# A decoder trunk on one core: three groups of two chunks per channel mixer computed as 2x2 block products in seven products

## The chip, the cores and the metric

The kernel runs on one core of a Trainium2 chip. The metric is the device time of one execution in microseconds (us); lower is better. Before the change the median of three runs is 585.55 us (585.5 to 585.72).

## The reference

Two layers over x (256 positions, 1024 channels). Each layer has a token mixer (layer 0: gated chunks, layer 1: block attention, both beside an attention into 256 memory tokens), then a channel mixer, each closed by a layer norm of 4^(1/4) x + f(x). The change concerns the channel mixer:

```
def swiglu(x, w_in, w_out):          # w_in: 1024 x 5632, w_out: 2816 x 1024
    g, u = jnp.split(x @ w_in, 2, axis=-1)
    return (jax.nn.silu(g) * u) @ w_out
```

All arrays are fp32.

## The kernel before

**Precision.** Every large product takes operands in two parts: hi, the value rounded to the matmul format, and lo, the rest. `split` (L142) makes them with one ScalarE cast (L143) and one VectorE subtraction (L144); the product is the sum of three passes, hi·hi, hi·lo and lo·hi.

**Weights.** `Stream` (L76) brings the weights in units of 128 partitions x 2048 columns (1 MB) in the fixed order of `weight_units` (L42): SyncE loads a unit into one of 3 raw buffers, `piece` (L101) splits it in steps of 512 columns into one of 5 split buffers, and a unit's buffer is free again when TensorE has used all of it. The buffers set how far ScalarE and VectorE may run ahead of TensorE.

**Channel mixer** (`Ffn`, L445). The 2816 hidden channels are 11 chunks of 256. For a chunk, gate (`g`) and value (`f`) are each computed with the weights as the stationary operand: `ws_wide` (L227) issues, for two column blocks and eight row blocks, one matmul of 512 columns (hi of the weight against hi and lo of x) and one of 256 (lo of the weight against hi of x), 32 in all. `projected` (L459) adds the two halves of the PSUM tile (L466, L467) and applies silu to the gate (L470); `chunk_in` (L473) multiplies (L476) and splits the result into `ht`. `chunk_out` (L512) multiplies `ht` with the chunk's output weights `w`, 24 matmuls of 512 columns into four PSUM accumulators, one chunk behind. In layer 1 the first two chunks have the positions on the partitions instead (`chunk_in_tm`, L481), half by half as x becomes ready.

**Order.** TensorE's instructions run in the order in which the program writes them. ScalarE, VectorE and SyncE get an order from the scheduler of the tile framework when the program is built, and each then runs its own list strictly in order. The main loop of layer 0 is

```
for c in range(NFF):
    ffn.chunk_in(c)
    if 1 <= c <= NFF - 3:
        ffn.chunk_out(c - 1)
```

Of the kernel before, what the change touches and what calls it, by code (L numbers as in the profile page):

```python
# [33 lines left out]
RAW_BUFS = 3  # L34
SPLIT_BUFS = 5
# [5 lines left out]

def weight_units():  # L42

    u = [(f"v{i}", 2 * W_MIX) for i in range(4)]
    u += [(n, 2048) for n in ("qm0", "u0", "u1", "u2", "km0", "vm0")]
    u += [(f"o0_{i}", 2048) for i in range(4)]
    u += [("km1", 2048), ("vm1", 2048)]
    u += ffn_units(0, 1)
    u += [(f"bv{i}", 2 * W_MIX) for i in range(4)]
    u += [("qm1", 2048)]  # L50
    u += [(f"qk{i}", 2048) for i in range(6)]
    u += [(f"o1_{i}", 2048) for i in range(4)]
    u += ffn_units(1, 1)
    return u


def ffn_units(l, ahead):

    u = []
    for c in range(NFF):  # L60
        u += [(f"g{l}_{c}", 2048), (f"f{l}_{c}", 2048)]
        if c >= ahead and c <= NFF - 3:
            u += [(f"w{l}_{c - ahead}", 2048)]
    u += [(f"w{l}_{c}", 2048) for c in range(NFF - 3, NFF)]
    return u
# [10 lines left out]
class Stream:  # L76


    def __init__(self, nc, rawp, splp, wflat, split, first):
        self.nc, self.rawp, self.splp, self.wflat, self.split = nc, rawp, splp, wflat, split  # L80
        self.units = weight_units()
        self.names = [n for n, _ in self.units]
        self.raw, self.hl = {}, {}
        self.loaded = self.split_u = first
        self.pos = 0
        self.finished = set()
        self.oldest = 0

# [4 lines left out]
    def load_ahead(self):  # L93
        while self.loaded < len(self.units) and self.loaded < self.split_u + RAW_BUFS:
            name, n = self.units[self.loaded]
            raw = self.rawp.tile([P, 2048], F32, tag="raw", name=f"raw_{name}")
# [4 lines left out]
    def piece(self):  # L101

        if self.split_u >= len(self.units) or self.split_u >= self.oldest + SPLIT_BUFS:
            return False
        self.load_ahead()
        name, n = self.units[self.split_u]
        if self.pos == 0:
            self.hl[name] = self.splp.tile([P, 2, 2048], F32R, tag="spl", name=f"spl_{name}")
        step = 512 if n == 2048 else 768
        hl, raw, c = self.hl[name], self.raw[name], self.pos  # L110
        self.split(hl[:, 0, c:c + step], hl[:, 1, c:c + step], raw[:, c:c + step])
        self.pos += step
        if self.pos == n:
            self.pos = 0
            self.split_u += 1
            self.load_ahead()
        return True

    def get(self, name):
        i = self.names.index(name)  # L120
        while self.split_u <= i:
            assert self.piece(), name
        return self.hl[name]

    def done(self, name):
        self.finished.add(name)
        while self.oldest < len(self.names) and self.names[self.oldest] in self.finished:
            self.oldest += 1


def build(nc, tc, ins, out):
    ET = mybir.EngineType
    with (
        tc.tile_pool(name="const", bufs=1) as const,
        tc.tile_pool(name="raw", bufs=RAW_BUFS) as rawp,
        tc.tile_pool(name="spl", bufs=SPLIT_BUFS) as splp,
# [27 lines left out]
        stream = Stream(nc, rawp, splp, ins["w"], split, first=4)  # L164

        def mm(o, lhsT, rhs, start, stop):
            nc.tensor.matmul(o, lhsT, rhs, start=start, stop=stop)  # L167
# [26 lines left out]
        for i in range(4):  # L194
            raw = rawp.tile([P, 2048], F32, tag="raw", name=f"raw_v{i}")
            hl = splp.tile([P, 2, 2048], F32R, tag="spl", name=f"spl_v{i}")
            for k in range(2):
                kk = 2 * i + k
                nc.sync.dma_start(xraw[:, kk, :], ins["xT"][kk * P:(kk + 1) * P, :])
                nh = 2 if kk == 0 else 1  # L200
                cuts = [(k * W_MIX + h * W_MIX // nh, k * W_MIX + (h + 1) * W_MIX // nh) for h in range(nh)]
                for c0, c1 in cuts:
                    nc.sync.dma_start(raw[:, c0:c1], stream.unit_ap(f"v{i}")[:, c0:c1])
                split(xT[:, kk, 0, :], xT[:, kk, 1, :], xraw[:, kk, :])
                for c0, c1 in cuts:
                    split(hl[:, 0, c0:c1], hl[:, 1, c0:c1], raw[:, c0:c1])
                w = hl[:, :, :2 * W_MIX].rearrange("p s (k c) -> p s k c", k=2)
                for h in range(2):
                    for n, (a, b) in enumerate(PASSES):
                        for tt in range(2):  # L210
                            mm(va[tt][h][:, :384], xT[:, kk, a, tt * P:(tt + 1) * P], w[:, b, k, h * 384:(h + 1) * 384],
                               kk == 0 and n == 0, kk == KT - 1 and n == 2)
            stream.done(f"v{i}")
# [4 lines left out]
        def ws_proj(pst, w, xs, cols=(0, 1)):  # L218

            wv = w.rearrange("p s (k c) -> p s k c", k=KT)  # L220
            for j in cols:
                for k in range(KT):
                    for n, (a, b) in enumerate(PASSES):
                        mm(pst[:, j % pst.shape[1], :], wv[:, a, k, j * P:(j + 1) * P], xs(b, k),
                           k == 0 and n == 0, k == KT - 1 and n == 2)

        def ws_wide(pst, w, xs, j):  # L227


            wv = w.rearrange("p s (k c) -> p s k c", k=KT)  # L230
            for k in range(KT):
                for b in ((0, 1) if k == 0 else (1, 0)):
                    mm(pst[:, :T] if b else pst, wv[:, b, k, j * P:(j + 1) * P],
                       xs(0, k) if b else flat(xs(slice(None), k)), k == 0 and b == 0, k == KT - 1 and b == 0)
# [38 lines left out]
        def transpose_x(tt, xres, xT_new, nm):  # L273
            for h in range(2):
                pt = mm_tile(f"pt{nm}{tt}{h}")
                for k in range(4):
# [3 lines left out]
                      pt.rearrange("p (k t) -> p k t", k=4))  # L280

# [60 lines left out]
        def mem_v(name, memx):  # L342

            w = stream.get(name)
            wv = w.rearrange("p s (k c) -> p s k c", k=KT)
# [3 lines left out]
            def part(tt):  # L349
                for k in range(KT):  # L350
                    ts_pass(t[:, tt, :], lambda a: memx(a, k), lambda b: wv[:, b, k, :], tt, k == 0, k == KT - 1)
# [32 lines left out]
        def proj_t(name, xs):  # L384
            t = mm_tile(f"h{name}").rearrange("p (j t) -> p j t", j=2)
            ws_proj(t, stream.get(name), xs)
# [34 lines left out]
        class OutProj:  # L421
# [4 lines left out]
            def term(self, tt, k):  # L426
                def rhs(b, c0, c1):
                    w = stream.get(f"o{self.l}_{k // 2}").rearrange("p s (k c) -> p s k c", k=2)
                    return w[:, b, k % 2, c0:c1]
# [15 lines left out]
        class Ffn:  # L445
            def __init__(self, l, xs, xres, nm):
                self.l, self.xs, self.xres, self.nm = l, xs, xres, nm
                self.hts, self.acc = {}, None
# [10 lines left out]
            def projected(self, unit, name):  # L459

                s = work_tile(f"s{name}")
                for j in range(2):
                    p = mm_tile(f"p{name}{j}")
                    ws_wide(p, stream.get(unit), self.xs, j)
# [3 lines left out]
                stream.done(unit)  # L468
                if unit[0] == "g":
                    nc.scalar.activation(s, s, AF.Silu)  # L470
                return s

            def chunk_in(self, c):  # L473
                l, nm = self.l, self.nm
                sg, su = (self.projected(f"{w}{l}_{c}", f"{n}{nm}{c}") for w, n in (("g", "g"), ("f", "u")))
                nc.vector.tensor_mul(sg, sg, su)  # L476
                ht = self.ht_tile(c)
                src = sg.rearrange("p (k t) -> p k t", k=2)
                split(ht[:, 0], ht[:, 1], src)

            def chunk_in_tm(self, c, tt, pt, part):  # L481

                name = f"{'gf'[part]}{self.l}_{c}"
                w = stream.get(name).rearrange("p s (k c) -> p s k c", k=KT)
                for k in range(KT):
                    ts_pass(pt[:, part * 256:part * 256 + 256], lambda a: self.xs(a, k), lambda b: w[:, b, k, :], tt,
# [19 lines left out]
            def term(self, c, k, tt):  # L506
                def rhs(b, c0, c1):
                    w = stream.get(f"w{self.l}_{c}").rearrange("p s (k c) -> p s k c", k=2)
                    return w[:, b, k, c0:c1]
                return lambda a: self.hts[c][:, a, k, tt * P:(tt + 1) * P], rhs  # L510

            def chunk_out(self, c, last=False):  # L512
                for tt in range(2):
                    for k in range(2):
                        acc_mms(self.acc[tt], *self.term(c, k, tt), c == 0 and k == 0, last and tt == 1 and k == 1)
                stream.done(f"w{self.l}_{c}")

            def end_tile(self, tt, mid=None):

                for c in range(NFF - 3, NFF - 1):  # L520
# [34 lines left out]
        stream.get("qm0")  # L555
# [9 lines left out]
        wsT = actp.tile([P, 2, D], F32, tag="xres", name="wsT").rearrange("p a c -> p (a c)")[:, :12 * P]  # L565
# [5 lines left out]
        bsB = actp.tile([P, 6, P], F32, tag="bsB", name="bsB")  # L571
        for j in range(2):
            nc.sync.dma_start(bsB[j * HD:(j + 1) * HD, :, :], ins["bs"][j:j + 1, :, :].to_broadcast([HD, 6, P]))

        qm = mem_q("qm0", xs)
        vn = actp.tile([P, 2, W_MIX], F32, tag="vbig", name="vn")
# [7 lines left out]
        for i in range(3):  # L584
            pu = mm_tile(f"pu{i}").rearrange("p (j t) -> p j t", j=2)
            ws_proj(pu, stream.get(f"u{i}"), xs)
# [17 lines left out]
        for jj in range(3):  # L604
# [7 lines left out]
            bias = bsB[:, 2 * jj:2 * jj + 2, :].rearrange("p (j o) t -> p j o t", o=1).to_broadcast([P, 2, 2, P])  # L612
# [28 lines left out]
        transpose_x(0, xres, x1T, "a")  # L641
# [3 lines left out]
        transpose_x(1, xres, x1T, "a")  # L645
        vm_part(1)
        ffn = Ffn(0, x_of(x1T), xres, "f")
        for c in range(NFF):
            ffn.chunk_in(c)
            if c == 1:  # L650
# [216 lines left out]
```

## Time and profile before

| | |
|---|---|
| median of 3 runs | 585.55 us |
| the profiled execution, its own time | 586.11 us |
| its span, first to last instruction | 584.4 us |
| TensorE matmul busy | 572.7 us (98%) |
| VectorE busy | 415.7 us (71%) |
| ScalarE busy | 331.8 us (57%) |
| moved by DMA | 110.55 MB, 189 GB/s mean |
| mean granted TensorE clock | 0.998 |

The profile is of one execution; 1.7 us of its own time lie outside the span. Busy time of an engine counts an instruction's whole length, and instructions of one engine may overlap at their ends. A chain is the work that ended last, followed back step by step to what released it.

### The profile page before, as it was taken

The page shows a single profiled execution, that of the slowest core. Times are in us where ns is not written, and L with a number is a line of the kernel's source. Part 1 is how long each engine was busy: PE and PEld are TensorE (multiplying, and loading weights), DVE is VectorE, ACT ScalarE, POOL GpSimd, SP SyncE. Part 2 cuts the span into 40 slices and gives each one's busy share as a digit, 9 for nine tenths or more (in the row PEclk, how much of TensorE's full clock was granted, in tenths as well). Part 3 has the DMA queues.
Part 4 walks back from the last instruction along what each step waited for, and adds up shares of the span by engine and source line. Part 5 has one row for each costly group of instructions (what it writes and reads, how often), then busy time and mean ns, then how long its engine had stood idle before and what let it go on. Part 6 is the DMA issues. An engine that isn't in the chain of part 4 may idle for free.

```text
span 584.4 us, 9071 instructions
## 1 busy us (share of the span) xinstructions
PE 572.7 (98%) x3496; PEld 508.4 (87%) x3496; DVE 415.7 (71%) x783; ACT 331.8 (57%) x718; POOL 14.7 (3%) x22
## 2 busy tenths in 40 slices
PE   7999999999999999999999999999999999999995
PEld 7999979888888888888999899789988888888884
DVE  5788989866556557565988887497766566566637
ACT  6767957755545545553468888464646455455410
POOL 1030000000000000000100000000000000000001
PEclk9999999999999999999999999999999999999999
DMA  8996557755545645545386324128735545555002
GB/s 295 354 347 247 189 219 242 288 201 201 216 165 195 216 170 190 173 151 181 117 297 236 131 87 145 73 72 283 290 149 215 182 179 216 183 180 180 34 1 72
DMA packets 19867, 110.55 MB, mean 189 GB/s; under 512 B 2160, under 2 KB 4976, under 8 KB 8432
## 3 DMA queue, kind: packets, MB, share of 16 engines
q1 hardware_dynamic: 19536, 109.72, 52.2%
q8 instruction: 27, 0.44, 0.3%
q10 hardware_dynamic: 288, 0.26, 0.1%
q14 instruction: 16, 0.13, 0.1%
HBM read 108.92 MB, written 1.05 MB: 188 GB/s over the span
## 4 chain that ended last, share of the span: by engine, by line
PE 95%; DVE 2%; DMA 1%; ACT 0%; issue 0%; SPq 0%; POOLq 0%
PE puf L167 11%; PE pgf L167 11%; PE fof L167 10%; PE fog L167 9%; PE pug L167 9%; PE pgg L167 9%; PE qk L167 5%; PE tm L167 4%; PE opc L167 4%; PE opa L167 4%; PE pu L167 3%; PE bv L167 3%; PE pvm L167 3%; PE va L167 2%; PE hqm L167 2%; PE hkm L167 2%
## 5 line engine op out<-in xcount | busy, mean ns | idle before, releaser
L143 ACT CAST spl_f<-raw_f 128x512 fp32r<-128x512 f32 x88 | 48.7, 619 | 43.6 <-issue 32.7
L144 DVE TENSOR_TENSOR spl_f<-raw_f,spl_f 128x512 fp32r<-128x512 f32 x88 | 55.5, 685 | 23.3 <-ACT spl_f L143 23.2
L167 PE MATMUL puf<-x1T,spl_f 128*128 128x256 f32 (+1 forms) x352 | 63.3, 337 | 0.0
L167 PE MATMUL pgf<-x1T,spl_g 128*128 128x256 f32 (+1 forms) x352 | 63.3, 337 | 0.0
L144 DVE TENSOR_TENSOR spl_w<-raw_w,spl_w 128x512 fp32r<-128x512 f32 x88 | 56.7, 688 | 7.1 <-ACT spl_w L143 5.6
L167 PE MATMUL fof<-spl_w,htf 128*128 128x512 f32 x264 | 61.6, 390 | 0.0
L167 PEld LDWEIGHTS pgf<-x1T,spl_g 128*128 128x128 f32 x352 | 54.4, 188 | 8.1
L167 PEld LDWEIGHTS puf<-x1T,spl_f 128*128 128x128 f32 x352 | 54.4, 188 | 7.9
L144 DVE TENSOR_TENSOR spl_g<-raw_g,spl_g 128x512 fp32r<-128x512 f32 x88 | 56.7, 686 | 4.1 <-ACT spl_g L143 3.5
L167 PEld LDWEIGHTS fof<-spl_w,htf 128*128 128x128 f32 x264 | 49.5, 188 | 10.0
L143 ACT CAST spl_w<-raw_w 128x512 fp32r<-128x512 f32 x88 | 49.8, 619 | 9.3 <-issue 5.0
L167 PE MATMUL fog<-spl_w,htg 128*128 128x512 f32 x228 | 53.2, 389 | 0.0
L143 ACT CAST spl_g<-raw_g 128x512 fp32r<-128x512 f32 x88 | 49.8, 621 | 5.0 <-PE tm L167 2.5
L167 PE MATMUL pgg<-x3T,spl_g 128*128 128x512 f32 (+1 forms) x288 | 51.9, 338 | 0.0
L167 PE MATMUL pug<-x3T,spl_f 128*128 128x512 f32 (+1 forms) x288 | 51.8, 337 | 0.0
L167 PEld LDWEIGHTS pgg<-x3T,spl_g 128*128 128x128 f32 x288 | 44.5, 188 | 6.6
L167 PEld LDWEIGHTS fog<-spl_w,htg 128*128 128x128 f32 x228 | 42.7, 188 | 8.6
L167 PEld LDWEIGHTS pug<-x3T,spl_f 128*128 128x128 f32 x288 | 44.5, 188 | 6.5
L167 PE MATMUL qk<-x2T,spl_qk 128*128 128x256 f32 x288 | 37.0, 285 | 0.0
L167 PEld LDWEIGHTS qk<-x2T,spl_qk 128*128 128x128 f32 x288 | 35.2, 191 | 0.6 <-issue 0.6
L466 ACT COPY sgf<-pgf 128x256 f32<-128x256 f32 x22 | 8.2, 373 | 29.3 <-PE pgf L167 29.3
L467 DVE TENSOR_TENSOR sgf<-sgf,pgf 128x256 f32<-128x256 f32 x22 | 9.3, 421 | 21.1 <-ACT sgf L466 20.9
(187 smaller groups left out, 893.3 us busy)
## 6 DMA issues: line engine op xcount, KB each, us to landing
raw_g<-in_w SPq DMA_DIRECT2D x22, 1024.0 KB, 4.9
raw_f<-in_w SPq DMA_DIRECT2D x22, 1024.0 KB, 4.8
raw_w<-in_w SPq DMA_DIRECT2D x22, 1024.0 KB, 4.8
raw_o<-in_w SPq DMA_DIRECT2D x8, 1024.0 KB, 4.9
raw_qk<-in_w SPq DMA_DIRECT2D x6, 1024.0 KB, 4.9
raw_u<-in_w SPq DMA_DIRECT2D x3, 1024.0 KB, 7.0
raw_bv<-in_w SPq DMA_DIRECT2D x4, 768.0 KB, 4.4
raw_v<-in_w SPq DMA_DIRECT2D x7, 384.0 KB, 5.3
```

The costliest lines, as they stand in the source:

```text
L143: nc.scalar.copy(hi, src)
L144: nc.vector.tensor_sub(lo, src, hi.bitcast(F32))
L167: nc.tensor.matmul(o, lhsT, rhs, start=start, stop=stop)
L466: nc.scalar.copy(sl, p[:, T:])
L467: nc.vector.tensor_add(sl, sl, p[:, :T])
```

## The change

Three times per channel mixer two chunks `c` and `c+1` form a group (`S` in the plan below; `P` is a chunk as before, `T` one of the two chunks of layer 1 with positions on the partitions). The group's left operand is x as 2x2 blocks (positions 0 to 127 and 128 to 255, channels 0 to 511 and 512 to 1023), its right operand the 1024 x 1024 weights as 2x2 blocks (gate and value columns): four raw units of 1 MB named 11, 12, 21, 22. Their product is formed in seven block products M1 to M7 instead of eight. Each is 12 matmuls in `product`, with x as the stationary operand and 512 weight columns moving.

- The left operands that are sums are made once per layer from fp32 copies of x (`transpose_x` keeps them, `sums` adds and splits).
- The right operands that are sums are made in `make`, in place in the raw unit, by VectorE, one half unit at a time, before the half is split: M5, M6, M7 and M4 take one addition per half.
- The products of a group come out with positions on the partitions, so its two `ht` tiles take eight TensorE transposes (step `tp`), run inside the next chunk.
- All weights are now split in halves of 1024 columns into 9 half buffers; a half is freed by itself. There are 4 raw buffers, and the units 11 and 21 lie in two activation tiles (`gb` and `vbig`) instead.
- The mixer's norm vectors are loaded at the last chunk (before: at chunk 4), since unit 11 uses their tile; layer 0's spatial bias comes with six transfers instead of two.
- TensorE's order in a mixer is the list that `ffn_steps` returns.

```
+RAW_BUFS = 4
+HALF_BUFS = 9
+PLAN = ((("P", 0), ("S", 1), ("P", 3), ("S", 4), ("P", 6), ("P", 7), ("S", 8), ("P", 10)),
+        (("T", 0), ("T", 1), ("S", 2), ("P", 4), ("S", 5), ("P", 7), ("S", 8), ("P", 10)))
+PRODUCTS = ("M1", "M5", "M2", "M3", "M6", "M7", "M4")
+OPERAND = {"M1": ("11", None), "M5": ("11", "12"), "M2": ("21", None), "M3": ("22", None),
+           "M6": ("11", "22"), "M7": ("12", "22"), "M4": ("21", "11")}
...
+def ffn_steps(l):
+    steps, prev = [], []
+    for kind, c in PLAN[l]:
+        outs = [("out", p, k, (0, 1)) for p in prev for k in range(2)]
...
+        if kind == "P":
+            ins = [("in", c, w, x) for w in "gf" for x in range(2)]
...
+            steps += [ins[0], ("tp",), ins[1], *outs[:n // 2], ins[2], *outs[n // 2:max(n // 2, n - 1)], ins[3],
+                      *outs[max(n // 2, n - 1):]]
+        else:
+            ins = [("s", c, m) for m in PRODUCTS]
+            steps += [*ins[:5], outs[0], ins[5], outs[1], ins[6]]
...
+    def make(self):
...
+        raw = self.raw[parts[0]][:, sl]
+        if len(parts) == 2:
+            self.nc.vector.tensor_add(raw, raw, self.raw[parts[1]][:, sl])
+        hl = self.splp.tile([P, 2, 1024], F32R, tag="spl", name="spl_" + "_".join(map(str, key)))
+        self.split(hl[:, 0, :n], hl[:, 1, :n], raw)
...
+            def sums(self, A):
+                a11, a12, a21, a22 = A[0, 0], A[0, 1], A[1, 0], A[1, 1]
+                nc.vector.tensor_sub(a22, a22, a21)
+                nc.vector.tensor_sub(a21, a11, a21)
+                nc.vector.scalar_tensor_tensor(a11, a11, -1.0, a22, ALU.mult, ALU.subtract)
+                nc.vector.scalar_tensor_tensor(a12, a12, -1.0, a11, ALU.mult, ALU.subtract)
...
+                    split(hl[0], hl[1], a)
...
+            def product(self, c, m):
...
+                dst = {"M1": self.X, "M6": self.X, "M7": self.X, "M4": self.X, "M2": self.Y}.get(m, self.Z)
...
+                for x in range(2):
+                    w = stream.get(f"s{self.l}_{c}", m, x)
+                    for k in range(2):
+                        for n, (a, b) in enumerate(PASSES):
+                            mm(dst, self.left[m](a, 2 * x + k), w[:, b, k * 512:(k + 1) * 512],
...
+                if m == "M1":
+                    self.m1 = kept("m1", self.X)
+                elif m == "M5":
+                    self.m5 = kept("m5", self.Z)
+                elif m == "M2":
+                    nc.vector.tensor_add(self.m1, self.m1, self.Y)
+                    nc.scalar.activation(self.m1, self.m1, AF.Silu)
+                elif m == "M6":
+                    u2 = kept("u2", self.X)
+                    nc.vector.tensor_add(u2, u2, self.Z)
+                    nc.vector.scalar_tensor_tensor(self.m1, self.m1, -1.0, u2, ALU.mult, ALU.mult)
+                elif m == "M7":
+                    nc.vector.tensor_add(self.m5, self.m5, self.X)
+                elif m == "M4":
+                    sg = work_tile(f"sg{self.nm}{c}")
+                    nc.scalar.activation(sg, self.X, AF.Silu)
+                    nc.vector.scalar_tensor_tensor(self.m5, self.m5, -1.0, sg, ALU.mult, ALU.mult)
...
         ffn = Ffn(0, x_of(x1T), xres, "f")
-        for c in range(NFF):
-            ffn.chunk_in(c)
...
+        stream.held.clear()
+        ffn.sums(A)
+        gb = ffn.run()
```

The order in which the engines' instructions stand moves with this. In the lists below `raw_` and `spl_` are the raw and split forms of a weight, with layer, chunk or group, product and half in the name (`spl_s0_1_M5_0`: layer 0, group 1, product M5, half 0; `raw_s0_1_11`: its unit 11); `Aa` are the fp32 copies of x, `Sf` their split sums, `sgf`, `sff`, `suf` gate and value of a chunk, `m1` and `m5` the two results of a group; a size ends the row.

VectorE before, where layer 0's channel mixer begins, from the last pieces of x on (L144 split, L467 addition of a projection's halves):

```order
L144 TENSOR_TENSOR x1T_1014<-pta11_1203,x1T_1014 128x4x128
L377 TENSOR_TENSOR klm_128<-hkm1_1087,kkm11_1086 64x256
L144 TENSOR_TENSOR spl_g0_1_1342<-raw_g0_1_1168,spl_g0_1_1342 128x512 x2
L144 TENSOR_TENSOR spl_f0_1_1393<-raw_f0_1_1246,spl_f0_1_1393 128x512 x4
L144 TENSOR_TENSOR spl_w0_0_1449<-raw_w0_0_1297,spl_w0_0_1449 128x512 x2
L467 TENSOR_TENSOR sgf0_1235<-sgf0_1235,pgf00_1236 128x256
```

VectorE now at the same place, after the first two sums of x (L219 split, L176 addition of two weight units, L540 and L541 the other sums of x, L555 addition of a projection's halves):

```order
L219 TENSOR_TENSOR spl_s0_1_M1_0_1342<-raw_s0_1_11_1234,spl_s0_1_M1_0_1342 128x1024
L540 SCALAR_TENSOR_TENSOR Aa00_1057<-Aa00_1057,Aa11_1185 128x512
L219 TENSOR_TENSOR SfM51_1217<-Aa11_1185,SfM50_1216 128x512
L541 SCALAR_TENSOR_TENSOR Aa01_1066<-Aa01_1066,Aa00_1057 128x512
L219 TENSOR_TENSOR SfM61_1225<-Aa00_1057,SfM60_1224 128x512
L219 TENSOR_TENSOR SfM71_1229<-Aa10_1176,SfM70_1228 128x512
L219 TENSOR_TENSOR SfM31_1221<-Aa01_1066,SfM30_1220 128x512
L555 TENSOR_TENSOR sgf0_1282<-sgf0_1282,pgf00_1232 128x256
L219 TENSOR_TENSOR spl_s0_1_M1_1_1351<-raw_s0_1_11_1234,spl_s0_1_M1_1_1351 128x1024
L555 TENSOR_TENSOR sgf0_1282<-sgf0_1282,pgf01_1233 128x256
L176 TENSOR_TENSOR raw_s0_1_11_1234<-raw_s0_1_11_1234,raw_s0_1_12_1236 128x1024 x2
L176 TENSOR_TENSOR raw_s0_1_12_1236<-raw_s0_1_12_1236,raw_s0_1_22_1240 128x1024
```

The four sums of x, their four splits and three weight additions now stand between x and the second product's weights.

VectorE now, around the end of layer 0's second group (L606 the addition of M7 into m5, L610 the last product of the group):

```order
L606 TENSOR_TENSOR m5f4_1756<-m5f4_1756,Xf4_1713 128x512
L219 TENSOR_TENSOR spl_g0_6_1_1937<-raw_g0_6_1699,spl_g0_6_1_1937 128x1024
L219 TENSOR_TENSOR spl_w0_4_0_1964<-raw_w0_4_1849,spl_w0_4_0_1964 128x1024
L219 TENSOR_TENSOR spl_w0_4_1_1979<-raw_w0_4_1849,spl_w0_4_1_1979 128x1024
L219 TENSOR_TENSOR spl_f0_6_0_1998<-raw_f0_6_1851,spl_f0_6_0_1998 128x1024
L219 TENSOR_TENSOR spl_w0_5_0_2017<-raw_w0_5_1863,spl_w0_5_0_2017 128x1024
L610 SCALAR_TENSOR_TENSOR m5f4_1756<-m5f4_1756,sgf4_1897 128x512
L219 TENSOR_TENSOR spl_f0_6_1_2032<-raw_f0_6_1851,spl_f0_6_1_2032 128x1024
```

Five splits of later weights stand ahead of the product that finishes the group. Before, a chunk's own product had no weights of this kind between it and the value projection: VectorE's rows there were

```order
L467 TENSOR_TENSOR suf2_1535<-suf2_1535,puf20_1536 128x256
L467 TENSOR_TENSOR suf2_1535<-suf2_1535,puf21_1566 128x256
L476 TENSOR_TENSOR sgf2_1484<-sgf2_1484,suf2_1535 128x512
L144 TENSOR_TENSOR spl_g0_4_1766<-raw_g0_4_1635,spl_g0_4_1766 128x512 x2
L144 TENSOR_TENSOR htf2_1586<-sgf2_1484,htf2_1586 128x512
```

## Rows read from the trace of the kernel before

**Rows 1.** The page: span, and busy time of each engine.

```profile
span 584.4 us, 9071 instructions
PE 572.7 (98%) x3496; PEld 508.4 (87%) x3496; DVE 415.7 (71%) x783; ACT 331.8 (57%) x718; POOL 14.7 (3%) x22
```

**Rows 2.** Busy time by stretch; columns: PE, PEld, DVE, ACT, POOL, PEclk, DMA share, GB/s.

```profile
102.40:286.20 183.80, 183.80 (x978) 157.61 (x977) 121.68 (x209) 96.94 (x194) 0.99 (x1) 1.00 0.53 189
391.70:415.00 23.30, 23.30 (x199) 23.30 (x198) 19.26 (x37) 12.28 (x24) 0.99 (x1) 1.00 0.69 242
```

**Rows 3.** The chain that ended last, layer 0's mixer: start, us, what.

```profile
98.69 0.87 PE pta L277 x8
...
102.43 5.59 PE pgf L167 x32
108.02 5.59 PE puf L167 x32
113.61 5.59 PE pgf L167 x32
...
124.80 5.44 PE fof L167 x24
```

**Rows 4.** The same chain where layer 1's mixer leaves its first two chunks.

```profile
416.23 5.47 PE fog L167 x24
421.70 0.22 PE tpg L500 x2
421.92 4.20 PE pgg L167 x24
```

**Rows 5.** VectorE in order of time: start, us, line, operation, count.

```profile
84.11 2.49 DVE L144 TENSOR_TENSOR spl_vm<-raw_vm,spl_vm 128x512 fp32r<-128x512 f32 x4
86.51 1.89 DVE L144 TENSOR_TENSOR spl_g<-raw_g,spl_g 128x512 fp32r<-128x512 f32 x3
...
288.05 0.94 DVE L144 TENSOR_TENSOR spl_bv<-raw_bv,spl_bv 128x768 fp32r<-128x768 f32 x1
288.91 0.20 DVE L262 BATCH_NORM_AGGREGATE mvf<-stf 128x2 f32<-128x12 f32 x1
...
290.97 1.41 DVE L269 SCALAR_TENSOR_TENSOR xres<-xres,rsf,gb0ffn 128x512 f32<-128x512 f32 x2
292.30 1.89 DVE L144 TENSOR_TENSOR spl_qm<-raw_qm,spl_qm 128x512 fp32r<-128x512 f32 x3
...
401.46 1.28 DVE L144 TENSOR_TENSOR x3T<-ptc,x3T 128x512 fp32r<-128x512 f32 x2
```

**Rows 6.** Groups of instructions, each shape apart: count, busy us, mean ns, idle before.

```profile
L144 DVE TENSOR_TENSOR spl_f<-raw_f,spl_f 128x512 fp32r<-128x512 f32 x88 | 55.5, 685 | 23.3 <-ACT spl_f L143 23.2
L467 DVE TENSOR_TENSOR sgf<-sgf,pgf 128x256 f32<-128x256 f32 x22 | 9.3, 421 | 21.1 <-ACT sgf L466 20.9
L476 DVE TENSOR_TENSOR sgf<-sgf,suf 128x512 f32<-128x512 f32 x11 | 7.6, 692 | 0.4
L144 DVE TENSOR_TENSOR spl_bv<-raw_bv,spl_bv 128x768 fp32r<-128x768 f32 x8 | 7.5, 954 | 0.7 <-ACT spl_bv L143 0.6
L143 ACT CAST spl_g<-raw_g 128x512 fp32r<-128x512 f32 x88 | 49.8, 621 | 5.0 <-PE tm L167 2.5 <-DVE x1T L144 0.7 <-DMA raw_g<-in_w 0.7
L143 ACT CAST spl_bv<-raw_bv 128x768 fp32r<-128x768 f32 x8 | 6.5, 835 | 9.7 <-issue 9.7
L353 ACT COPY svm<-pvm 128x512 f32<-128x512 f32 x2 | 1.2, 594 | 0.3 <-PE pvm L167 0.3
```

**Rows 7.** ScalarE in order of time, the last casts ahead of layer 0's mixer.

```profile
101.83 0.37 ACT L376 CAST kkm<-hkm 64x256 fp32r<-64x256 f32 x1
```

**Rows 8.** The page's DMA issues: count, KB each, us to landing.

```profile
raw_g<-in_w SPq DMA_DIRECT2D x22, 1024.0 KB, 4.9
```

More of the change, by code (lines that the diff above doesn't have):

```diff
@@ L33 @@
 WARM = 30
-RAW_BUFS = 3
-SPLIT_BUFS = 5
+RAW_BUFS = 4
+HALF_BUFS = 9
 NFF = D_FF // 256
@@ L65, in ffn_units, with columns @@
+def columns(name):
+    return 2 * W_MIX if name[0] == "v" and name[1] != "m" or name[0] == "b" else 2048
+def weight_units():
+    u = []
+    for k in weight_halves():
+        names = [k[0]] if len(k) == 2 else [f"{k[0]}_{q}" for q in OPERAND[k[1]] if q]
+        u += [(n, columns(n)) for n in names if (n, columns(n)) not in u]
     return u
@@ L93, in load_ahead @@
     def load_ahead(self):
-        while self.loaded < len(self.units) and self.loaded < self.split_u + RAW_BUFS:
+        while self.loaded < len(self.units):
             name, n = self.units[self.loaded]
-            raw = self.rawp.tile([P, 2048], F32, tag="raw", name=f"raw_{name}")
+            tag = TAGS.get(name[-2:]) if name[0] == "s" else None
+            if tag:
+                if tag in self.held:
+                    return
+                self.held.add(tag)
+                raw = self.actp.tile([P, 2, D], F32, tag=tag, name=f"raw_{name}").rearrange("p a c -> p (a c)")
+            else:
+                if len(self.ring) >= RAW_BUFS and self.left[self.ring[-RAW_BUFS]]:
+                    return
+                self.ring.append(name)
+                raw = self.rawp.tile([P, 2048], F32, tag="raw", name=f"raw_{name}")
             self.nc.sync.dma_start(raw[:, :n], self.unit_ap(name))
@@ L99, in load_ahead, with get, rows, done @@
             self.loaded += 1
-    def piece(self):
-        if self.split_u >= len(self.units) or self.split_u >= self.oldest + SPLIT_BUFS:
-            return False
+    def make(self):
+        key = self.keys[self.made]
+        assert self.made < self.oldest + HALF_BUFS, key
         self.load_ahead()
[L106 to L127, printed above, removed]
+        parts = self.parts(key)
+        n = columns(parts[0]) // 2
+        sl = slice(key[-1] * n, key[-1] * n + n)
+        raw = self.raw[parts[0]][:, sl]
+        if len(parts) == 2:
+            self.nc.vector.tensor_add(raw, raw, self.raw[parts[1]][:, sl])
+        hl = self.splp.tile([P, 2, 1024], F32R, tag="spl", name="spl_" + "_".join(map(str, key)))
+        self.hl[key] = hl
+        self.split(hl[:, 0, :n], hl[:, 1, :n], raw)
+        for p in parts:
+            self.left[p] -= 1
+            if not self.left[p] and p[0] == "s" and p[-2:] in TAGS:
+                self.held.remove(TAGS[p[-2:]])
+        self.made += 1
+        self.load_ahead()
+    def get(self, *key):
+        i = self.keys.index(key)
+        while self.made <= i:
+            self.make()
+        return self.hl[key]
+    def rows(self, name, k, n):
+        h = self.get(name, 2 * k // n)
+        c = columns(name) // n
+        return h[:, :, k % (n // 2) * c:(k % (n // 2) + 1) * c]
+    def done(self, *key):
+        for k in [key] if len(key) > 1 else [(key[0], 0), (key[0], 1)]:
+            self.finished.add(k)
+        while self.oldest < len(self.keys) and self.keys[self.oldest] in self.finished:
             self.oldest += 1
@@ L162, in flat, with mm @@
             return s.rearrange("p a b -> p (a b)") if len(s.shape) == 3 else s
-        stream = Stream(nc, rawp, splp, ins["w"], split, first=4)
-        def mm(o, lhsT, rhs, start, stop):
-            nc.tensor.matmul(o, lhsT, rhs, start=start, stop=stop)
+        stream = Stream(nc, rawp, actp, splp, ins["w"], split, first=4)
+        def mm(o, lhsT, rhs, start, stop, on=False):
+            nc.tensor.matmul(o, lhsT, rhs, start=start, stop=stop, skip_group_check=on)
         va = [[acc_tile(f"va{tt}{h}") for h in range(2)] for tt in range(2)]
@@ L280, in transpose_x @@
                       pt.rearrange("p (k t) -> p k t", k=4))
+                if keep is not None:
+                    keep[tt, h] = work_tile(f"A{nm}{tt}{h}")
+                    nc.scalar.copy(keep[tt, h], pt)
         def load_gb(l, which):
@@ new lines, in transposes @@
+            def transposes(self):
+                if not self.pending:
+                    return
+                c, hs = self.pending
+                self.pending = None
+                for j in range(2):
+                    tp = mm_tile(f"tp{self.nm}{c + j}").rearrange("p (k t) -> p k t", k=2)
+                    for k in range(2):
+                        for tt in range(2):
+                            nc.tensor.transpose(tp[:, k, tt * P:(tt + 1) * P],
+                                                hs[tt][:, (2 * j + k) * P:(2 * j + k + 1) * P], ident)
+                    ht = self.ht_tile(c + j)
+                    split(ht[:, 0], ht[:, 1], tp)
@@ new lines, in run @@
+            def run(self):
+                for st in ffn_steps(self.l):
+                    if st[0] == "in":
+                        self.chunk_in(*st[1:])
+                        if st[1:] == (NFF - 1, "g", 0):
+                            stream.held = {"gb", "vbig"}
+                            self.gb = load_gb(self.l, "ffn")
+                    elif st[0] == "s":
+                        self.product(*st[1:])
+                    elif st[0] == "tp":
+                        self.transposes()
+                    else:
+                        self.chunk_out(*st[1:])
+                return self.gb
```

245 lines of the change are left out of this document (142 added, 103 removed).

## The prediction

> **What bounds the kernel now.** I read the page's busy times first, then busy time by stretch, then the chain that ended last, then VectorE in order of time. TensorE is busy for 572.7 of 584.4 us [rows 1], and in layer 0's channel mixer for 183.80 of 183.80 us, where VectorE has 121.68 and ScalarE 96.94 [rows 2]. The chain there is TensorE and nothing else: 5.59 us for 32 matmuls of a gate or value projection, 5.44 us for 24 matmuls of output weights, each starting when the last one ends [rows 3]. The reader should see that a matmul taken away here is time taken away, as long as the other engines stay ahead. VectorE has slack in the mixer's middle, but little where a mixer begins: 19.26 of 23.30 us in layer 1's first two chunks [rows 2]. The granted clock is 1.00 in both stretches.
>
> **TensorE: what goes and what comes.** Two chunks' gate and value took 4 x 5.59 = 22.36 us [rows 3]. A group takes 7 products of 12 matmuls of 512 columns, 84. The nearest rows are those of the output weights, with the same shape and the same operand roles: 24 in 5.44 us, 0.227 each, so 19.04 us. The eight transposes of a group cost as much as eight of x, 0.87 us [rows 3]. A group saves 22.36 - 19.04 - 0.87 = 2.45 us, six groups **14.7 us**. The output matmuls and the other chunks are the same, only in halves.
>
> **VectorE: the price of an instruction.** Four splits of 512 columns began at 84.11, the next work at 86.51: 0.60 us each from start to start, though one lasts 0.685 [rows 5, 6]. One of 768 took 0.86 (288.05 to 288.91) [rows 5]. So 256 columns add 0.26: I take 1.12 for 1024 columns and 0.34 for 256. A scalar-tensor-tensor of 512 takes 0.66 (two from 290.97 to 292.30) [rows 5]. No row has an addition of two raw units; a product of two SBUF tiles lasts 0.692, a split 0.685 [rows 6], so it is priced like a split.
>
> **VectorE in a group.** Before, four units needed no additions. A group has 14 half splits, 8 half additions and 2 halves of output weights, 24 x 1.12 = 26.9, with 5 x 0.60 and 2 x 0.66 for its results: 31.2 us, beside 24.48 on TensorE (M1, M5, M2, M3, M6, w, M7, w, M4, nine steps of 2.72). It can only keep up if it enters a group some 7 us ahead. A group with the following chunk and four halves of output weights is 24.48 + 22.93 = 47.4 us on TensorE (22.93 is four halves of 2.80, 0.87, four of 2.72), and 32 x 1.12 + 7 x 0.60 + 2 x 0.66 + 4 x 0.34 = 42.7 on VectorE. So the lead is won back in the next chunk, and what counts is how VectorE enters the first group.
>
> *Layer 0, first group.* The last fp32 copies of x are made on ScalarE after the casts that end at 102.20 [rows 7], two of 0.594 [rows 6], to 103.4. From there to the split of M4's first half VectorE's list has 23 instructions of 1024 columns (15 splits, 8 additions), 11 of 512, 3 scalar-tensor-tensors and 4 of 256: 25.8 + 6.6 + 2.0 + 1.4 = 35.7 us, to 139.1. TensorE starts the group at 113.61 as the second chunk did [rows 3] and wants that half 8 x 2.72 = 21.76 later, at 135.4. It waits about 3.7, first seen at M6; with hand-overs **4.0 us**. The cause is the sums of x, their splits and three weight additions ahead of M5.
>
> *Its second group.* The step to look at is the last product (L610), which stands behind five splits; the transposes wait for it and the rest of TensorE's list waits behind them. From 139.1 there are 39 of 1024, 7 of 512, 2 and 4: 50.6 us, and 0.75 for itself: 190.4. TensorE wants it at 113.61 + 4.0 + 24.48 + 22.93 + 24.48 + 2.80 = 192.3. Nothing, with 1.9 us to spare. The third group comes after a chunk without additions and is safer.
>
> *Layer 1.* VectorE starts on the second half of x at 401.46 [rows 5]. To the last product of its first group are 31 of 1024, 11 of 512, 3 and 7: 34.7 + 6.6 + 2.0 + 2.4 = 45.7, and 0.75: 447.9. TensorE enters the group at 421.92 [rows 4] and wants it 27.28 later, at 449.2. Only 1.3 to spare, and VectorE's list has waits on TensorE's PSUM tiles in it; I put **0.5 us**. The later groups follow at 42.7 against 47.4.
>
> **At nothing.** *ScalarE:* 620 ns for 512 columns and 835 for 768 [rows 6] make about 1.05 for 1024; 24 of these in 47.4 us, with some 7 us of copies, casts and silu, are 32: VectorE covers it, and without that cover it would still not reach TensorE. *DMA:* the units are as many and as large, 9 MB in 47.4 us, and one lands in 4.9 us [rows 8]. Units 11 and 21 wait on SyncE until the last group's M4 is summed, and `g0_7` is queued behind those of the third group; it then lands some 5 to 10 us later, while TensorE has a 22.93 us chunk to run first. If that cover went, the delay would show in full. *PSUM:* M6, M3, M7 and M4 add onto a tile that must have been copied; each copy (0.594) has a step of 2.72 between. *End of a mixer:* the last chunk's `ht` is 0.37 [rows 7], 0.42, 0.69, 0.62 and 0.69 [rows 6], 2.8 us, behind its value projection; three half steps of 1.36 us, 4.1, still run first. The norm's vectors now load in the last chunk, with its 11.2 us and the closing products ahead of their use. *The bias's six transfers:* early in layer 0, where the chain does not wait for DMA. *Halves of 1024 instead of pieces of 512:* 0.08 us less VectorE time per half, in stages where TensorE does not wait.
>
> **Sum.** The profiled execution took 586.11 us: 586.11 - 14.7 + 4.0 + 0.5 = 575.9. The median of the runs is 0.56 lower: **575.4 us**, 1.7% faster. Bounds of the unknown: no wait at all gives 585.55 - 14.7 = 570.9; the upper bound is in the rivals.
>
> **Rivals.** *VectorE priced at whole instructions.* If additions and splits that alternate did not overlap their ends as the splits of one unit do [rows 5], each would cost its length: 1.23 (1024), 0.69, 0.75, 0.42. The first group's list is then 39.6 us, a wait of 7.6; the second's 55.8, a wait of 3.6; layer 1's 50.7, a wait of 3.7; after that 47.2 against 47.4. Waits of 14.9 eat the 14.7: 585.8 us, no change. Against it: in the rows start to start is 0.60 also between different lines. The Trainium skill (VectorE: DVE Perf Modes, "The DRAIN you can't avoid") says that the next operation does not start until the pipe is empty, which would make this the time; the trace here disagrees, with 0.60 us from start to start for instructions of 0.685.
>
> *The weight sums run as a chain* (slower). A summed half is addition, cast on ScalarE, split; if VectorE sat idle for the cast (1.05) in all eight, a group would cost it 8.4 us more: the first wait grows to 12.4, layer 1's to 7.1, and each of the four others gets about 51.1 against 47.4, 3.7: some 34 us of waits and about 605 us. It decides from about 5 us per group, five casts in the open (9 + 3.7 + 4 x 0.3 = 13.9, near the 14.7). For it: VectorE did wait 23.2 us for the casts of `spl_f` [rows 6]. Against it: its list has the additions of M6 and M7 ahead of the splits, so ScalarE has its input early.
>
> *The seven products' waits vanish:* if ScalarE's and VectorE's lists fit better than summed, 570.9.
>
> **How the numbers follow.** A measurement of this kernel can tell about 0.2%, 1.2 us, from no change. Forecast, 573 to 579: 0.58. No waits, near 571: 0.09. Part of the VectorE losses, 579 to 584: 0.13. Whole instructions, about 586: 0.07. Chain of sums, slower: 0.13. Faster is the first three, 0.80; no change 0.07; slower 0.13. A range of 571 to 584 leaves out the last two cases, 0.2.
>
> **What would show it.** Right: products of 2.72 us in the chain, tiles X, Y, Z in place of gate and value; TensorE waiting for VectorE at M6 of layer 0's first group and hardly elsewhere; VectorE near 500 us busy; its 1024-column instructions 1.2 us long and 1.12 apart. Wrong: waits of over 1 us in each of the six groups, at transposes that wait for L610, or at M7 and M4; products slower than 2.72; the clock below 1.00 in the mixers; raw units landing after ScalarE asks for them.

## The result and the profile after

| | before | after |
|---|---|---|
| median | 585.52 us (585.12 to 585.72, 4 runs) | 578.33 us (578.09 to 578.87, 4 runs) |
| ratio, 95% interval | | 0.9879 [0.9862, 0.9896] |
| profiled execution; its span | 586.11; 584.4 us | 578.25; 576.5 us |

Faster by 7.2 us, where the forecast was 10.1. The page of the changed kernel, beside [rows 1]: TensorE lost 10.5 us of work, VectorE gained 80.

```profile
span 576.5 us, 8502 instructions
PE 562.2 (98%) x3280; PEld 493.2 (86%) x3280; DVE 496.0 (86%) x675; ACT 357.6 (62%) x562; POOL 13.7 (2%) x22
```

TensorE's waits (for whom, us in total, times, longest; lines left out are marked):

```profile
PE Xf L242 <- DVE spl_s_M L219: 1.8, 1, 1.8
...
PE Xf L242 <- ACT spl_s_M L218: 0.9, 1, 0.9
...
PE ptm L404 <- DVE pm L384: 0.7, 1, 0.7
```

In the mixers only one place is new, the tile X of layer 0's first group. (The wait at `ptm`, at 71.5 us, is new too but costs nothing there: the first mixer begins at 102.34, before at 102.43.) TensorE in order of time shows the group's beginning, M1 into X; M5 into Z, M2 into Y and M3 into Z follow:

```profile
113.61 2.93 PE L242 MATMUL Xf<-spl_s_M,x1T 128*128 128x512 f32 x12
```

The chain from there on (start, us, what):

```profile
122.73 0.60 DVE m1f L599
123.33 3.40 DVE raw_s L176 x3
126.73 1.15 DVE spl_s_M L219
127.88 0.04 issue
127.93 4.33 PE Xf L242 x11
132.26 2.78 PE fof L242 x12
135.04 2.72 PE Xf L242 x12
...
140.48 2.85 PE Xf L242 x12
143.33 2.81 PE pgf L242 x16
```

Each product takes 2.72 to 2.85, except M6. M6 is `Xf x11`; the first of its 12 matmuls ran during the wait. At 113.61 + 2.77 + 3 x 2.72 = 124.54 TensorE wanted M6. Its split ended at 127.88, behind three weight additions, so it is 3.4 us late, less the one matmul that ran meanwhile: 3.2. But M6 is also slow in itself: 11 matmuls in 4.33 us, where 0.227 each make 2.49. The stretches show why (columns: length, PE busy with its instructions, PEclk, DMA share, GB/s):

```profile
124.50:126.00 1.50, 0.56 (x2) 1.00 0.00 0
126.00:127.90 1.90, 0.15 (x1) 1.00 0.09 34
127.90:129.00 1.10, 1.07 (x4) 0.91 0.73 223
129.00:132.20 3.20, 3.20 (x9) 0.50 0.57 238
132.20:135.00 2.80, 2.80 (x14) 1.00 0.00 0
```

Between 124.5 and 127.9 TensorE was idle for 2.7 us by these rows (1.50 - 0.56 and 1.90 - 0.15). M6 resumed at 127.93, and about 1 us later the granted clock fell to 0.50, the lower of its two levels (1.2 GHz); by 132.2 it was back at 1.00. M6 ended at 132.26 instead of 127.26 (124.54 + 2.72), **5.0 us** late: 1.8 from the clock, 3.2 from VectorE.

VectorE's large instructions, each shape apart (count, busy us, mean ns, idle before):

```profile
L219 DVE TENSOR_TENSOR spl_s_M<-raw_s,spl_s_M 128x1024 fp32r<-128x1024 f32 x84 | 100.8, 1220 | 4.0 <-ACT spl_s_M L218 3.6
L176 DVE TENSOR_TENSOR raw_s<-raw_s,raw_s 128x1024 f32<-128x1024 f32 x48 | 56.9, 1219 | 0.0
```

They last 1.22 us; in the chain three additions take 3.40, 1.13 from start to start. The forecast had 1.12.

### The profile page after: what moved, and what is told of

Read it like the earlier page. It is cut to its first block, busy times and chain, and to the rows that moved or that the text cites. A ratio compares the mean times of both kernels' runs of the same rounds, so it can differ in the third digit from the quotient of the medians.

```text
span 576.5 us, 8502 instructions
## 1 busy us (share of the span) xinstructions
PE 562.2 (98%) x3280; PEld 493.2 (86%) x3280; DVE 496.0 (86%) x675; ACT 357.6 (62%) x562; POOL 13.7 (2%) x22
## 4 chain that ended last, share of the span: by engine, by line
PE 75%; DVE 8%; ACT 1%; issue 1%; POOLq 0%; DVEq 0%
PE fof L242 10%; PE fog L242 9%; PE Xg L242 6%; PE qk L242 6%; PE Xf L242 5%; PE tm L242 4%; PE opc L242 4%; PE pgf L242 4%; PE pff L242 4%; PE pgg L242 3%; PE pfg L242 3%; PE bv L242 3%; PE Zg L242 3%; PE Zf L242 2%; DVE spl_s_M L219 2%; PE last L242 1%
## 5 line engine op out<-in xcount | busy, mean ns | idle before, releaser
L218 ACT CAST spl_s_M<-raw_s 128x1024 fp32r<-128x1024 f32 x84 | 87.2, 1053 | 42.0 <-DVE raw_s L176 19.7
L219 DVE TENSOR_TENSOR spl_s_M<-raw_s,spl_s_M 128x1024 fp32r<-128x1024 f32 x84 | 100.8, 1220 | 4.0 <-ACT spl_s_M L218 3.6
L242 PE MATMUL fof<-spl_w,htf 128*128 128x512 f32 x264 | 63.1, 391 | 0.0
L219 DVE TENSOR_TENSOR spl_w<-raw_w,spl_w 128x1024 fp32r<-128x1024 f32 x44 | 53.6, 1221 | 6.2 <-ACT spl_w L218 5.9
L242 PEld LDWEIGHTS fof<-spl_w,htf 128*128 128x128 f32 x264 | 49.7, 189 | 10.4
L176 DVE TENSOR_TENSOR raw_s<-raw_s,raw_s 128x1024 f32<-128x1024 f32 x48 | 56.9, 1219 | 0.0
L242 PE MATMUL fog<-spl_w,htg 128*128 128x512 f32 x228 | 54.6, 391 | 0.0
L218 ACT CAST spl_w<-raw_w 128x1024 fp32r<-128x1024 f32 x44 | 45.8, 1049 | 9.4 <-PE pff L242 1.8
L242 PEld LDWEIGHTS fog<-spl_w,htg 128*128 128x128 f32 x228 | 42.7, 188 | 8.8
L242 PE MATMUL qk<-x2T,spl_qk 128*128 128x256 f32 x288 | 37.0, 285 | 0.0
L242 PEld LDWEIGHTS qk<-x2T,spl_qk 128*128 128x128 f32 x288 | 35.2, 191 | 0.6 <-DVE klm L454 0.4
L242 PE MATMUL pgf<-x1T,spl_g 128*128 128x256 f32 (+1 forms) x160 | 29.7, 340 | 0.0
L242 PE MATMUL pff<-x1T,spl_f 128*128 128x256 f32 (+1 forms) x160 | 29.3, 339 | 0.0
L242 PEld LDWEIGHTS pff<-x1T,spl_f 128*128 128x128 f32 x160 | 25.0, 188 | 3.8
L242 PEld LDWEIGHTS pgf<-x1T,spl_g 128*128 128x128 f32 x160 | 24.8, 189 | 3.5
L219 DVE TENSOR_TENSOR spl_f<-raw_f,spl_f 128x1024 fp32r<-128x1024 f32 x20 | 24.2, 1215 | 2.9 <-ACT spl_f L218 2.6
L219 DVE TENSOR_TENSOR spl_g<-raw_g,spl_g 128x1024 fp32r<-128x1024 f32 x20 | 24.2, 1220 | 2.2 <-ACT spl_g L218 2.0
L242 PE MATMUL opc<-spl_o,mix 128*128 128x512 f32 x96 | 23.5, 397 | 0.0
L242 PE MATMUL opa<-spl_o,mix 128*128 128x512 f32 x96 | 22.5, 392 | 0.0
L242 PE MATMUL Xf<-spl_s_M,SfM 128*128 128x512 f32 x72 | 19.2, 418 | 2.7 <-DVE spl_s_M L219 1.8
```

The costliest lines, as they stand in the source:

```text
L176: self.nc.vector.tensor_add(raw, raw, self.raw[parts[1]][:, sl])
L218: nc.scalar.copy(hi, src)
L219: nc.vector.tensor_sub(lo, src, hi.bitcast(F32))
L242: nc.tensor.matmul(o, lhsT, rhs, start=start, stop=stop, skip_group_check=on)
```

## Experiments

Each ran beside the kernel before, whose median was 585.5 to 585.6 us. The theory: TensorE waits once, in layer 0's first group, because VectorE enters it without a lead (work done ahead of what TensorE needs), and the clock adds to that wait. Rivals: the wait is made inside a group, by addition, cast and split; VectorE pays whole lengths; the rest of the missing gain lies in the halves.

### A chunk more ahead of the first group

```
-PLAN = ((("P", 0), ("S", 1), ("P", 3), ("S", 4), ("P", 6), ("P", 7), ("S", 8), ("P", 10)),
+PLAN = ((("P", 0), ("P", 1), ("S", 2), ("P", 4), ("S", 5), ("P", 7), ("S", 8), ("P", 10)),
```

> One number of the table is moved: layer 0 runs chunks 0 and 1 alone and its first group is chunks 2 and 3; three groups as before. Theory (TensorE waits in the first group because VectorE enters it without a lead): a chunk alone gives VectorE some 10 us of lead, so the wait at M6 (3.4 us idle) and the eleven matmuls at half clock behind it (1.8 us) both go: 578.3 - 5.2 = about 573.2 us. Rival (the wait is made inside a group, by addition, cast on ScalarE and split of each summed half): it moves with the group, 578.3 us.

The diff changes one row of the table: layer 0's first and second group each stand one chunk later. Measured: 573.60 us, ratio 0.9793 [0.9778, 0.9808]; 4.7 us less than the change. The chain, where the first group now stands:

```profile
130.58 2.72 PE Xf L242 x12
...
138.74 2.72 PE Zf L242 x12
141.46 2.72 PE Xf L242 x12
```

M6 (141.46) follows M3 at once. The same additions, casts and splits stand in the group, and TensorE waits for none of them: the lead was missing, not the group's own speed. The rival of hand-overs falls.

### Without the sums of x

```
-        ffn.sums(A)
+        for m in ("M5", "M3", "M6", "M7"):
+            tt, h = {"M5": (1, 1), "M3": (0, 1), "M6": (0, 0), "M7": (1, 0)}[m]
+            ffn.left[m] = lambda a, k, tt=tt, h=h: x1T[:, 4 * h + k, a, tt * P:(tt + 1) * P]
...
```

> Layer 0's channel mixer leaves out the four sums and differences of x, their casts and splits and the four fp32 copies; products M5, M3, M6 and M7 take plain blocks of x as left operands instead. VectorE has 2 x 0.60 + 2 x 0.66 + 4 x 0.60 = 4.9 us less ahead of M6. Theory (VectorE's list ahead of M6 sets the wait): M6's split ends near 123.0 us where TensorE wants it at 124.6, no idle time, no half clock: about 573.2 us. Rival (hand-overs inside the group set it): 578.3 us.

Measured: 573.59 us, ratio 0.9794 [0.9779, 0.9809]. With the group where the change put it, M6 begins on time:

```profile
122.17 2.72 PE Zf L242 x12
124.89 2.72 PE Xf L242 x12
```

So with a shorter VectorE list the wait goes, as the forecast's list said. The run takes away more than the 4.9 us that it was meant to: VectorE's order changed with it, and the group's ninth split, M6's first half, ended at 121.88, 6.0 us earlier than in the change, where 3.2 had to go. ScalarE's casts of these sums and the fp32 copies went too; this run alone does not part these, but the run with a chunk more kept all of them and did not wait.

### The wait filled with matmuls

```
+                if (self.l, c, m) == (0, 1, "M6"):
+                    busy = mm_tile("busy")
+                    for i in range(14):
+                        mm(busy, self.xs(0, 0)[:, :P], flat(self.xs(slice(None), 0)), True, True)
```

> Fourteen matmuls of 512 columns with a result that nobody reads are put ahead of M6 in layer 0's first group, 14 x 0.227 = 3.2 us, where TensorE had 3.4 us of idle time. Theory (the idle time made the granted clock fall to 0.50, and M6's eleven slow matmuls cost 4.33 - 2.49 = 1.8 us): no half clock, about 576.5 us though the wait itself stays. Rival (M6's matmuls were slow for another reason, such as late operands): 578.3 us or a little more.

Measured: 577.06 us, ratio 0.9858 [0.9839, 0.9877], 1.3 us below the change. The chain, and the same stretch as above (columns as there):

```profile
114.41 2.77 PE Xf L242 x12
...
125.36 3.17 PE busy L242 x14
128.53 2.81 PE Xf L242 x12
131.34 2.72 PE fof L242 x12
```

```profile
127.90:129.00 1.10, 1.10 (x6) 1.00 0.06 22
129.00:130.00 1.00, 1.00 (x6) 1.00 0.78 295
130.00:131.00 1.00, 1.00 (x6) 1.00 1.07 451
131.00:132.20 1.20, 1.20 (x7) 1.00 0.62 253
```

M6 takes 2.81 at a clock of 1.00. From M1's start it ends after 16.93 us (131.34 - 114.41), in the change after 18.65: 1.7 us, the expected size. In this profile the mixer began 0.8 later, which the medians may share. By the medians alone the 1.3 us are not clear of the noise, since the two intervals overlap; it is the trace that decides. M6 still comes late, its operands are the same, and with the gap filled its matmuls run at 1.00: the half clock was the idle time's doing, and the rival of late operands falls. The Trainium skill (TensorE: Matmul & The Clock Gate, Part 1) says that the clock is gated by recent activity; the runs here agree.

### Halves without groups

```
-PLAN = ((("P", 0), ("S", 1), ("P", 3), ...
+PLAN = (tuple(("P", c) for c in range(11)),
+        (("T", 0), ("T", 1), *(("P", c) for c in range(2, 11))))
...
-        ffn.sums(A)
```

> No group at all: every chunk's gate and value as plain projections, no sums of x, but weights in halves, the four raw tiles and the new order of loads are kept. The forecast put halves at nothing: 585.5 us. Rival (the halves cost the 1.5 us by which the change fell short of 14.7 - 5.2 elsewhere: steps of 2.82 in place of 2.80, the attention stage 0.35 and the tail 0.26 longer): about 586.5 to 587 us.

Measured: **590.17 us**, ratio 1.0078 [1.0064, 1.0092]: worse than either. Everything in the change other than the groups, costed at nothing, costs 4.6 us, and in the mixers TensorE waits for nothing. The chain (the kernel's line numbers are two higher here, L244 for L242):

```profile
120.03 2.77 PE fof L244 x12
122.80 5.64 PE pff L244 x32
128.44 2.77 PE fof L244 x12
131.21 5.64 PE pgf L244 x32
```

A chunk's steps take 5.64, 2.77, 5.64, 2.77 us, 16.82 in all; before it was 5.59, 5.59, 5.44 [rows 3], 16.62. In layer 0's mixer (first `pgf` to first `bv`) that makes 1.7 us, in layer 1 (first `tm` to first `last`) 1.5; the attention stage between the mixers is 0.4 longer, the tail (from layer 1's last pieces to the end) 0.5, and the first mixer began 0.7 later. This start differs from profile to profile (102.3 to 103.2 over the runs).

### Halves in the order of before

On the version without groups:

```
-            steps += [ins[0], ("tp",), ins[1], *outs[:n // 2], ins[2], *outs[n // 2:max(n // 2, n - 1)], ins[3],
-                      *outs[max(n // 2, n - 1):]]
+            cut = 1 if c == NFF - 1 else 0
+            steps += [ins[0], ins[1], ("tp",), *outs[:cut], ins[2], ins[3], *outs[cut:]]
...
         def ws_wide(psts, w, xs, x):
+            if x == 0:
+                return
             for j, pst in enumerate(psts):
-                for k in range(KT // 2 * x, KT // 2 * (x + 1)):
+                for k in range(KT):
```

> On the version without groups (590.2 us): the weights stay in halves, but TensorE works as before the change, a projection's 32 matmuls tile by tile and the 24 of the output weights in a row. Theory (each change from one kind of step to another costs TensorE about 0.05 us, and halves double these changes: 5.64 in place of 5.59 and 2.77 in place of 2.72): 590.2 - 2 x (22 x 0.045 + 20 x 0.05) = about 586.2 us. Rival (the smaller tiles or their hand-overs cost it, whatever the order): 590 us.

Measured: 587.43 us, ratio 1.0034 [1.0021, 1.0047]. The chain:

```profile
130.93 5.59 PE pgf L244 x32
136.52 5.59 PE pff L244 x32
142.11 5.44 PE fof L244 x24
```

The steps are back at their old durations with the tiles still halves, so in the mixers the order cost it, not the tiles. The mixers take what they took before (183.79 and 177.19 us), 3.2 us less than in the last run, where the expectation had counted 4.0. The span is still 1.3 us longer than before the change, outside them: 0.4 in the attention stage, 0.3 in the tail, 0.7 in the start of this profile. What makes the attention stage and the tail longer was not tried; the stage takes 105.8 us instead of 105.5 in every version with halves, with groups or without. The other 0.6 of the medians' 1.9 is that the profiled execution of before stood 0.56 above its median.

### Only the two output halves together

The same `steps` as in the last run, with `ws_wide` left in halves.

> On the version without groups (590.2 us): only the two output halves of a chunk are put next to each other; the projections stay in half steps (both tiles for half of the rows, then both for the other half). Theory of the changes of kind: the second output half of each chunk goes from 2.77 to 2.72, some 18 x 0.05 = 0.9 us: 589.3 us, the rest of the cost being in the projections' half steps. Rival (it is the alternation of projections and outputs alone): 586 to 587 us, as with the joined order.

Measured: 589.77 us, ratio 1.0074 [1.0063, 1.0085]. The chain:

```profile
130.50 5.64 PE pgf L244 x32
...
141.77 5.49 PE fof L244 x24
```

By the medians this is not told from 590.17; by the chain the two mixers (as above) take 185.08 and 178.27 us against 185.50 and 178.64, 0.8 less, as expected. The 24 matmuls of the outputs now take 5.49 (2.77 + 2.72). The rest lies in the projections' half steps, still 5.64, where TensorE goes from tile to tile twice as often. Why a change of tile or kind costs some 0.02 to 0.05 us stays open.

### Four more VectorE instructions per group

On the version with a chunk more ahead:

```
             self.nc.vector.tensor_add(raw, raw, self.raw[parts[1]][:, sl])
+            if key[-1] == 0:
+                self.nc.vector.tensor_tensor(raw, raw, raw, ALU.max)
```

> On the version with a chunk more ahead of the first group (573.6 us): four more VectorE instructions of 1024 columns in each group, a maximum of a summed half with itself. Theory (1.12 us from start to start, so 42.7 + 4 x 1.12 = 47.2 us of VectorE per group and chunk beside 47.4 on TensorE): the later groups still fit, and only layer 1's first group, with 1.3 us to spare by the forecast's sum, waits some 3 us: 574 to 577 us. Rival (VectorE pays whole lengths, 47.2 us per period already, 52.1 with four more): about 4.7 us in each of at least four groups, 592 us or more.

Measured: 582.14 us, ratio 0.9941 [0.9928, 0.9954]: 8.5 us more, between the two. By the chains layer 0's mixer lost 2.1 us and layer 1 7.4, at tile X in four of the six groups. VectorE in order of time, layer 0's third group (line numbers two higher again; L178 is the added maximum):

```profile
234.15 0.69 DVE L601 TENSOR_TENSOR m1f<-m1f,Yf 128x512 f32<-128x512 f32 x1 [0.32 <-PE Yf L244]
234.75 2.35 DVE L221 TENSOR_TENSOR spl_s_M<-raw_s,spl_s_M 128x1024 fp32r<-128x1024 f32 x2
237.03 1.22 DVE L221 TENSOR_TENSOR spl_w<-raw_w,spl_w 128x1024 fp32r<-128x1024 f32 x1
...
245.04 0.68 DVE L608 TENSOR_TENSOR m5f<-m5f,Xf 128x512 f32<-128x512 f32 x1
245.64 1.22 DVE L178 TENSOR_TENSOR raw_s<-raw_s 128x1024 f32<-128x1024 f32 x1
248.02 2.36 DVE L221 TENSOR_TENSOR spl_s_M<-raw_s,spl_s_M 128x1024 fp32r<-128x1024 f32 x2 [1.17 <-ACT spl_s_M L220]
```

The price holds (two in 2.28, 1.14 each), so the rival of whole lengths falls. What fails is that a lead could be saved up over a whole period. L601 needs M2's result: VectorE stands still for it for 0.32 us, and what stands behind it cannot start sooner. From 234.15 to the split of M4's half, which ends at 249.26, VectorE needs 15.1 us, 1.2 of it waiting for that half's cast; TensorE runs five steps between M2 and M4, 13.6 us. So the margin is that stretch's, not the period's 4.7. Most of the excess of 1.5 is the cast: the added maximum stands between addition and cast, and nothing is left in the list to cover the cast with.

In layer 1's third group the clock falls as well. M4 there waits 1.8 us (0.8 to 1.2 in the three other groups), and behind it the granted clock is 0.50 from 542.0 to 544.4; in the other groups it stays at 1.00. The chain at M4, first in layer 0's third group, then in layer 1's:

```profile
249.30 2.79 PE Xf L244 x11
...
540.36 4.04 PE Xg L244 x11
544.41 3.14 PE pgg L244 x16
```

Eleven matmuls take 4.04 us instead of 2.79, and the gate step behind them 3.14 instead of 2.81: some 1.6 of the 8.5 us are the clock's.

### The best version

First I put the joined order (each projection whole, a chunk's output matmuls in a row) on the version with a chunk more ahead, with the diff of the halves in the order of before:

> The version with a chunk more ahead of the first group, with the joined order in the chunks alone; the groups as they are. Theory of the changes of kind: some 0.09 to 0.29 us in each of eight chunks, 1.7 us in all: 573.6 - 1.7 = about 571.9 us. Rival: 573.6 us, or more where a projection now needs both its halves 1.4 us earlier and VectorE is late.

Measured: 574.52 us, ratio 0.9811 [0.9799, 0.9824], a loss. The chain where layer 0's last chunk begins:

```profile
249.85 5.61 PE pgf L242 x32
...
255.75 0.83 ACT spl_bv L218
256.59 0.50 ACT htf L218
257.08 0.04 issue
257.13 1.87 PE fof L242 x6
```

The transposes (not shown on this chain) now stand behind the whole gate projection, with the first output step right after. It waits for its `ht`, whose cast stands behind one of a weight. Between the end of the gate (249.85 + 5.61 = 255.46) and 257.13 go 1.7 us, 0.87 of them the transposes and 0.8 idle; then six matmuls take 1.87 us, where the version with a chunk more took 1.40. That is 1.3 us lost, and 0.5 in layer 1 at the same place. So the last chunk keeps its half steps:

```
+            if c == NFF - 1:
+                steps += [ins[0], ("tp",), ins[1], outs[0], ins[2], ins[3], outs[1]]
+            else:
+                steps += [ins[0], ins[1], ("tp",), ins[2], ins[3], *outs]
...
```

> The version with a chunk more ahead of the first group, with projections and outputs joined in all chunks but the last of a layer, which keeps its half steps. Theory (the joined order saves the changes of kind, 0.6 us up to layer 0's last chunk and 0.3 us in layer 1 by the last run's chain, and lost more than that in the last chunks, where the transposes had been moved behind a whole projection and the first output step waited for their cast): 573.6 - 0.9 = about 572.7 us. Rival (the joined order loses by VectorE's order elsewhere too): 573.6 us or more.

> The version with a chunk more ahead of the first group once more, beside the joined one on the same chip: 573.6 us.

Measured, on one chip: **572.68 us**, ratio 0.9778 [0.9765, 0.9792], and 573.63 us, 0.9798 [0.9784, 0.9811], for the version with the chunk alone, both as expected. The joined one was 572.24 to 572.76 in five runs, the other 573.58 to 574.13 in four. In the joined version's layer 0 TensorE is busy throughout (columns: PE, PEld, DVE, ACT, POOL, PEclk, DMA share, GB/s):

```profile
102.50:279.13 176.63, 176.63 (x870) 149.11 (x870) 162.84 (x182) 112.98 (x145) 0.99 (x1) 1.00 0.51 188
```

## Why the prediction was right, and where it was not

**Right: TensorE's bill.** Products took 2.72, tiles X, Y, Z stood in place of gate and value, and the eight transposes took 0.87. From the first group of layer 1 to its last pieces the time went from 146.95 to 139.98 us: 6.97 saved of 7.35.

**Right: where it waits, and why.** M6 of layer 0's first group, from VectorE's list; two runs that lengthen the lead or shorten the list remove it. The forecast summed VectorE's list to M4's first half; the whole wait stood at M6, and behind it M7 and M4 took 2.72 and 2.85. No wait at layer 1's first group, where 0.5 was put.

**Mis-sized: "It waits about 3.7 ... with hand-overs 4.0 us".** It was 5.0. VectorE's part was 3.2, less than summed: at the forecast's prices the list to M6's split is 24.9 us and it took 25.3, but it began at 102.56 and not at 103.4. The other 1.8 came from the clock, which fell behind the wait. The forecast counted a wait at its own length; "the clock below 1.00 in the mixers" stood only among the signs.

**Wrong: "Halves of 1024 instead of pieces of 512: 0.08 us less VectorE time per half, in stages where TensorE does not wait".** Only VectorE was costed, and the steps of TensorE were taken as "the same, only in halves"; but the halves also change TensorE's order. Without groups the halves and what came with them cost 4.6 us, 3.2 of them by the order in the mixers. With groups fewer half steps are left, since products and outputs follow each other at 2.72, and the chains show 1.75: 0.76 in layer 0's mixer (171.02 us from M1 to `bv`, where 172.61 - 7.35 + 5.0 = 170.26 was due), 0.38 in layer 1, 0.35 in the attention stage, 0.26 in the tail. That the order makes the 0.76 and 0.38 is argued from the steps of the chain (2.81 and 2.83 for a gate of 5.59); what makes the other 0.6 is open.

**The miss of 2.9 us.** The first wait was 1.0 longer than forecast, the halves and what came with them cost 1.75, and layer 1's wait of 0.5 did not come. The other 0.64 come from the profiled executions: before, it stood 0.56 above the median, and the forecast took the same off after; there it stood 0.08 below.

**Rivals.** Whole instructions: 1.13 and 1.14 us from start to start against 1.22 long, here and with four more. (At its own price of 1.23 this rival's sums are 0.2 us short, 39.8 for 39.6; nothing hangs on that. And the forecast's "0.60 also between different lines" is shown in its rows only for splits of L144; for different lines of the program the chain after shows it, from L599 at 122.73 to L176 at 123.33.) The Trainium skill's page that the forecast named (VectorE: DVE Perf Modes, "The DRAIN you can't avoid") adds that a next operation that is not held starts earlier, and the trace agrees with that. Chain of sums: VectorE waited 3.6 us in all for the casts of these splits, where the rival had 8.4 in each group, and with the lead TensorE waits for no cast; a cast came into the open only with four more instructions. No waits: 570.9 was forecast; without the wait the same groups gave 573.6, and in joined order 572.7. The difference to 570.9 is mostly what the halves and what came with them still cost, about 1.7 by the chain.

**Only by luck.** VectorE's slack in later groups was read from a period (42.7 against 47.4 us). The later groups did keep up, but the margin is smaller than that, as the run with four more showed.

## What to carry to other kernels

An engine that gets new work needs a lead where the work begins, so put the first such block a step later before making the block cheaper: one row of a table gave 4.7 us. Cost a change of granularity on every engine whose order it alters, above all on the one that bounds the kernel, and run that part alone. The lead of an engine that runs its list in order reaches only to its next instruction that waits for the other engine (here L601); sum its list from there, not over the period.

## What the runs showed of the hardware

The granted clock went from 1.00 to 0.50 after one gap with 2.7 us of idle time, and that cost 1.8 us more; matmuls without use in the gap kept it at 1.00. In the run with four more instructions it went to 0.50 after a gap with 1.8 us of idle time, and stayed at 1.00 after three with 0.8 to 1.2. And the same 32 matmuls took 5.59 us tile by tile and 5.64 in half steps, the same 24 took 5.44 in a row and 2 x 2.77 in two steps between projections, with no wait in the trace; why is open.
